# Two-layer encoder trunk: row norm ahead of the MLP's joins, sums that begin with the residual, operand differences on the vector engine

## The chip, the cores and the metric

One core of a Trainium2 chip runs the whole program. The metric is the device time in microseconds (us) of one execution. The engines are TensorE (PE, with its weight load PEld), VectorE (DVE), ScalarE (ACT), GpSimd (POOL) and SyncE (SP, which issues the DMAs).

## The reference

A trunk of two layers over a sequence of 1024 tokens with 1024 channels, all float32:

```
per layer:
  h = RMSNorm(x);  z = h @ W_in
  mix = concat[ attention(z), gated recurrence(z), conv module(z) ]
  x = x + mix @ W_out
  x = x + relu(RMSNorm(x) @ W1)^2 @ W2        # W1: 1024x4096, W2: 4096x1024
RMSNorm(x) = x * rsqrt(mean(x*x) + 1e-6) * gain
```

The change touches the last line only, the MLP.

## The kernel before, in words

**Arithmetic.** Tiles have channels on the 128 partitions and tokens along the row. Each float32 operand of a matmul is split into a high part (ACT, a rounding copy) and a low part (DVE, operand minus high part); `parts` does both (L900 to 910). A product takes three passes (high-high, high-low, low-high), so a product of one 128x512 result over four 128-row steps is 12 matmuls of 128x512.

**Two halves.** The MLP of a layer is done with seven products M1 to M7 in place of eight, in the manner of Strassen. The first half (x to hidden) runs 16 pairs p of hidden tiles times seven products in the order M1, M5, M2, M3, M6, M4, M7 (`product`, matmul L1009); the first two pairs are interleaved. The second half (hidden to output) runs 4 groups sg times seven stages in the order M1, M2, M5, M6, M3, M7, M4, and each stage four output tiles dt of 12 matmuls (matmul L1217). Both halves hold 28 x 48 = 1344 matmuls of 128x512.

**Operand sums and differences.** Before they are split, operands are combined: `sub` (L918), `add` (L915) and the sum for M5 in `parts` (L906) run on POOL; four differences of x per product M5 and M6 run on DVE. The functions are `x_parts` and `w_split`.

**Joins.** In the first half, `join` adds two partial results (DVE, L1018), then ACT does Relu (L1019) and Square (L1020). For pairs 12 to 15 DVE then multiplies with the row norm (`scaled`, L996). Differences t1, t2 (DVE) and t3, t4 (POOL) of the results are stored to memory with them (`store_half`, L921), for the second half to read back.

**Row norm.** The square of the norm's inverse can be taken out of relu(.)^2, so `sum_rows` (all-ones matmul L271) is called behind product 18 and its reciprocals behind products 40 to 47, and the hidden tiles of pairs 0 to 11 are not scaled: their sums are, in group sg 2 of the second half, on POOL (L996), where POOL also adds the residual (L915), which `residual` (L1157) fetches into buffers "m".

**Second half.** `load2` (L1063) loads W2 tiles, `load_a` (L1070) the stored activations, `collect` takes results out of PSUM: the first of each accumulator an ACT copy, the others a DVE add (L1194).

**What sets the order.** A scheduler orders instructions on each engine by program order, priority and its own costs, and gives any free buffer of a pool (14 buffers "m", 16 "xs", 8 "x", 4 "tmp"). Inside `ordered`, instructions of an engine are held in the order of the program: separate chains "a" (ACT), "v" (DVE), "p" (POOL) at the start of the first half, and a new chain from 4 products before its end through the second half; in between there is none. Parts are made 4 products (later 4 to 8 tiles) ahead of the matmuls.

Of the kernel before, what the change touches and what calls it, by code (L numbers as in the profile page):

```python
# [17 lines left out]
P = 128  # L18
# [27 lines left out]
def tile_hybrid_trunk(  # L46
# [128 lines left out]
    def flip(w, half):  # L175
        b = pse()
# [51 lines left out]
    def norm_stats(ssq):  # L228
        sp = pse()
# [5 lines left out]
        for h in range(2):  # L235
            nc.scalar.activation(rb[:, h * 512 : (h + 1) * 512], flip(w, h), AF.Copy)
        return rc, rb

    class Norm:
# [22 lines left out]
        def done(self):  # L262
            self.rc, self.rb = norm_stats(self.ssq)
            return self.rc, self.rb

        def sum_rows(self):
            all_ones = tmp((P, P))
            nc.gpsimd.memset(all_ones, 1.0)
            for half in halves(self.ssq):
                s = pse()  # L270
                nc.tensor.matmul(s, all_ones, half, start=True, stop=True)  # L271
                nc.scalar.activation(half, s, AF.Copy)
            return self.ssq
# [21 lines left out]
    for l in range(DEPTH):  # L295
# [574 lines left out]
        norm = Norm(lambda k: None, sp_.t([P, L], "Rb"))  # L870
# [62 lines left out]
        def x_parts(name):  # L933
# [8 lines left out]
            elif name == "M5":  # L942
                BC[name] = []
                for kt in R4:
                    nc.vector.tensor_tensor(B[1][kt], B[2][kt], B[1][kt], op=ALU.subtract)
                    BC[name].append(parts(B[1][kt], b_t()))
            elif name == "M3":
                BC[name] = [parts(B[4][kt], m_t()) for kt in R4]
            elif name == "M6":
                for kt in R4:  # L950
                    sub(B[2][kt], B[4][kt], B[2][kt])
                    nc.vector.tensor_tensor(B[4][kt], B[4][kt], B[1][kt], op=ALU.subtract)
# [8 lines left out]
        def w_split(name, a11, a12, a21, a22, box):  # L961
            if name == "M3":
                sub(a12, a12, a11)
            src = {"M1": a11, "M2": a12, "M5": (a21, a22), "M6": a11, "M3": a12, "M4": a22, "M7": a21}[name]
            both = parts(src, box)
            if name == "M5":
                sub(a21, a11, a21)
                sub(a11, a22, a21)
            return both
# [25 lines left out]
        def scaled(eng, dst, src, h):  # L995
            eng.tensor_tensor(dst, src, r2[:, h * 512 : (h + 1) * 512], op=ALU.mult)  # L996

        def product(p, name):
# [17 lines left out]
            def join(m, h, a, b):  # L1016
                o = d["o"][m][:, h * 512 : (h + 1) * 512]
                nc.vector.tensor_tensor(o, a, b, op=ALU.add)  # L1018
                nc.scalar.activation(o, o, AF.Relu)  # L1019
                nc.scalar.activation(o, o, AF.Square)  # L1020
                if p >= NPAIR - SG:
                    scaled(nc.vector, o, o, h)
                return o

            with tc.high_priority() if p == NPAIR - 1 else nullcontext():
# [3 lines left out]
                elif name == "M2":  # L1029
                    d["o"] = [spare(p), spare(p)]  # L1030
                    store_half(p, "M1", join(0, 0, bank, d["m1"]))
# [4 lines left out]
                elif name == "M6":  # L1036
                    b11, b12 = halves(d["o"][0])
                    join(0, 1, bank, d["m1"])
# [17 lines left out]
        seq = [(p, n) for n in ORDER[:5] for p in range(2)] + [(p, n) for p in range(2) for n in ORDER[5:]]  # L1056
# [9 lines left out]
        def load_a(sg, name):  # L1066
            for h in range(2):
                t = m_t() if sg > 0 or name not in ("M1", "M2") else b_t() if name == "M1" else tmp()
# [31 lines left out]

# [205 lines left out]
```

## Time and profile before

| | |
|---|---|
| median of 3 runs | 2584.42 us (2583.92 to 2586.57) |
| profiled execution | 2586.23 us, span 2584.3 us |
| PE busy in the span | 95% |
| DVE, ACT, POOL busy | 76%, 50%, 45% |
| MLP, first half, layers 0 and 1 | 318.29 and 318.35 us |
| MLP, second half, layers 0 and 1 | 324.66 and 325.79 us |
| mean granted clock in these | 0.97 to 0.99 |

The halves run from one first matmul to the next half's (the last one to its last matmul). Besides its 1344 matmuls each holds a few others. The profile counts an engine as busy while it executes, not while it waits for a semaphore.

### The profile page before, as it was taken

Reading aid. Unit: us, or ns where it says so; the run is one execution under the profiler, and the core shown is the slowest. Engines: PE = TensorE matmul, PEld = TensorE weight load, DVE = VectorE, ACT = ScalarE, POOL = GpSimd, SP = SyncE. Lnnn points to the kernel's source line nnn. Section 1 sums busy time; section 2 is a strip of 40 time slices with the busy share of each in tenths; the row PEclk is TensorE's granted clock in tenths of the full one; section 3 lists DMA queues with packets and bytes.
Section 4 is the critical chain, followed back from the end, with each engine's and each line's share of the span. In section 5 each row is a group of like instructions: output and inputs, shape, how many; then the busy total and the mean of one; then the engine's idle time right before and its main releaser. Section 6 shows DMA issues by size and latency. Waiting matters only on the chain. (4 is left out here: it accounts for less than half of the span.)

```text
span 2584.3 us, 34195 instructions
## 1 busy us (share of the span) xinstructions
PE 2463.8 (95%) x12568; PEld 2026.7 (78%) x12568; DVE 1971.8 (76%) x2725; ACT 1291.1 (50%) x2118; POOL 1159.5 (45%) x735
## 2 busy tenths in 40 slices
PE   8989999999999999999899899999998999999998
PEld 7767788878788887888787777888786888878886
DVE  6998589862865578899859985998628655788996
ACT  4222478763655555433423225777636555554322
POOL 0232566533644434357423325664346354343581
PEclk9999999999999999999999999999999999999999
DMA  4101300032244457445231112000323443664343
GB/s 162 52 33 59 106 24 18 26 128 93 91 162 147 163 186 245 134 144 172 101 109 44 48 61 96 17 22 22 133 88 118 147 163 139 217 219 156 113 163 122
DMA packets 115127, 287.01 MB, mean 111 GB/s; under 512 B 11408, under 2 KB 11664, under 8 KB 114960
## 3 DMA queue, kind: packets, MB, share of 16 engines
q1 hardware_dynamic: 114960, 284.83, 32.1%
q8 instruction: 99, 1.62, 0.3%
q14 instruction: 68, 0.56, 0.1%
HBM read 197.75 MB, written 87.03 MB: 110 GB/s over the span
## 5 line engine op out<-in xcount | busy, mean ns | idle before, releaser
L223 PE MATMUL S<-xs,whi 128*128 128x512 f32 x1280 | 363.6, 405 | 10.0 <-ACT xs L208 8.5
L223 PEld LDWEIGHTS S<-xs,whi 128*128 128x128 f32 x1280 | 243.1, 193 | 66.2 <-ACT xs L208 8.5
L908 ACT ACTIVATE xs<-m 128x512 fp32r<-128x512 f32 x216 | 125.8, 620 | 206.4 <-issue 52.7
L909 DVE TENSOR_TENSOR xs<-m,xs 128x512 fp32r<-128x512 f32 x216 | 207.3, 984 | 18.7 <-ACT xs L908 18.7
L769 POOL TENSOR_SCALAR P<-P,mx 128x1024 f32<-128x1024 f32 x124 | 143.0, 1153 | 164.6 <-DVE mx L768 122.1
L223 PE MATMUL S<-xs,wlo 128*128 128x512 f32 x640 | 203.0, 398 | 0.0
L1217 PE MATMUL S<-xs,xs 128*128 128x512 f32 x816 | 200.5, 389 | 0.0
L795 DVE TENSOR_TENSOR PT<-c,PT 128x512 fp32r<-128x512 f32 x256 | 170.9, 683 | 23.6 <-ACT PT L794 22.0
L794 ACT ACTIVATE PT<-c 128x512 fp32r<-128x512 f32 x256 | 147.5, 593 | 69.3 <-PE c L790 66.2
L199 ACT ACTIVATE whi<-raw 128x1024 fp32r<-128x1024 f32 x56 | 59.1, 1057 | 246.1 <-PE S L223 233.2
L1217 PEld LDWEIGHTS S<-xs,xs 128*128 128x128 f32 x816 | 153.2, 188 | 31.8
L811 PE MATMUL e<-PT,x 128*128 128x256 f32 x1024 | 173.2, 299 | 1.6 <-ACT PT L794 1.3
L764 DVE TENSOR_SCALAR_CACHE_REDUCE P<-S,nqc 128x1024 f32<-128x1024 f32 x124 | 158.4, 1278 | 16.1 <-PE S L753 7.2
L360 DVE SCALAR_TENSOR_TENSOR x<-x,par,x 128x1009 f32<-128x1009 f32 (+14 forms) x120 | 166.5, 1387 | 1.8
L790 PE MATMUL c<-cons,P 128*128 128x128 f32 x992 | 152.1, 277 | 10.4 <-POOL P L769 5.3
L753 PE MATMUL S<-x,QS 128*128 128x512 f32 x480 | 155.6, 423 | 4.7 <-DVE P L764 4.5
L1217 PE MATMUL c<-xs,xs 128*128 128x512 f32 x552 | 143.1, 405 | 13.3 <-DVE x L1194 13.1
L767 ACT ACTIVATE P<-P,mx 128x1024 f32<-128x1024 f32 x124 | 142.5, 1149 | 24.2 <-DVE P L764 22.7
L811 PEld LDWEIGHTS e<-PT,x 128*128 128x128 f32 x1024 | 139.5, 193 | 10.3 <-ACT PT L794 3.7
L1217 PE MATMUL e<-xs,xs 128*128 128x512 f32 x552 | 137.5, 391 | 9.7 <-DVE xs L909 6.6
L790 PEld LDWEIGHTS c<-cons,P 128*128 128x128 f32 x992 | 115.3, 141 | 36.3 <-issue 10.5
L223 PEld LDWEIGHTS S<-xs,wlo 128*128 128x128 f32 x640 | 122.6, 192 | 26.8 <-issue 0.3
(314 smaller groups left out, 5960.4 us busy)
## 6 DMA issues: line engine op xcount, KB each, us to landing
m<-ad SPq DMA_DIRECT2D x104, 512.0 KB, 3.9
ad<-x SPq DMA_DIRECT2D x176, 256.0 KB, 2.1
raw<-w_in_t SPq DMA_DIRECT2D x40, 512.0 KB, 3.4
xs<-w_t SPq DMA_DIRECT2D x36, 512.0 KB, 3.8
raw<-w_t SPq DMA_DIRECT2D x36, 512.0 KB, 3.5
m<-w_t SPq DMA_DIRECT2D x32, 512.0 KB, 4.9
ad<-tmp SPq DMA_DIRECT2D x48, 256.0 KB, 2.0
x<-w_t SPq DMA_DIRECT2D x24, 512.0 KB, 5.7
```

Of the source, the lines that this page charges most:

```text
L223: nc.tensor.matmul(zp[h] if type(zp) is list else zp[:, h, :], w, xx[:, h * 512 : (h + 1) * 512], start=first, stop=last)
L360: nc.vector.scalar_tensor_tensor(y[:, lo:hi], u[:, lo + d : hi + d], par[:, l, wof + tap : wof + tap + 1], y[:, lo:hi], op0=ALU.mult, op1= ...
L753: nc.tensor.matmul(S[:, hb, :], qs, kk[:, hb * 512 : (hb + 1) * 512], start=first, stop=not first)
L764: nc.vector.tensor_scalar(Pt, S, nqc[:, j, ci : ci + 1], 3.0e38, op0=ALU.mult, op1=ALU.min, accum_out=mx[:, 1:2])
L767: nc.scalar.activation(Pt, Pt, AF.Exp, bias=mx[:, 1:2], scale=-1.0, accum_out=mx[:, 2:3])
L769: nc.gpsimd.tensor_scalar(Pt, Pt, mx[:, 3:4], 0.0, op0=ALU.mult, op1=ALU.add)
L790: nc.tensor.transpose(t[:, q * P : (q + 1) * P], Pt[:, hb, q * P : (q + 1) * P], ident)
L794: nc.scalar.activation(hi, src, AF.Copy)
L795: nc.vector.tensor_tensor(lo, src, hi.bitcast(F32), op=ALU.subtract)
L811: nc.tensor.matmul(pvp[:, cs], VS[g][:, hb * 4 + kb, :], pt[:, kb, :], start=hb == 0 and n == 0, stop=hb == 1 and n == 7,)
L909: ordered("v", nc.vector.tensor_tensor(lo, src, hi.bitcast(F32), op=ALU.subtract))
L1217: nc.tensor.matmul(banks[dt], w[i][:, dt * P : (dt + 1) * P], a[j], start=n == 0 and name not in ("M6", "M7", "M3"), stop=n == 3 * SG - 1, ...
```

## The change

- The row norm is computed at the start of the first half: `norm.square` of the last x tile on DVE behind product 0, `norm.done` behind product 2. That is eight small column sums on PE (written in two parts, 16 matmuls of 128x1), 12 DVE operations of 128x8, an ACT widening, 8 PE transposes and 2 ACT copies into the tile `Rb`. `sum_rows`, the reciprocals and `scaled` are gone.
- A join is now a DVE add, a DVE `scalar_tensor_tensor` (max with 0, times `Rb`) and an ACT Square; the Relu is gone. For M2 of pairs 0 and 1 the second and third step come later, at M6.
- The accumulators of the second half are loaded with the residual (`load_acc`, 8 tiles of 0.5 MB), four behind the last but one product of the first half and four at the start of the second; every `collect` is a DVE add, and the POOL scaling and adding in sg 2 is gone.
- `add` and `sub` run on the engine in `row[0]`: DVE for the first 11 products, POOL up to 14 products before the first half's end, DVE from there and through the second half. They stand in the DVE chain "v" with the low parts. t3 and t4 follow `row[0]`.
- The two interleaved pairs at the start come in another order: M1 M1 M5 M5, then M2 M3 of pair 0, M2 M3 of pair 1, M6 M6, M4 M7, M4 M7.
- In group 0 of the second half the activations of M2 lie in buffers "xs", where they lay in "tmp".

```diff
-            if type(src) is tuple:
-                s = tmp((P, 512))
-                ordered("p", nc.gpsimd.tensor_tensor(s, *src, op=ALU.add))
-                src = s
...
+        row = [nc.vector]
...
-            nc.gpsimd.tensor_tensor(dst, a, b, op=ALU.add)
+            ordered("v", row[0].tensor_tensor(dst, a, b, op=ALU.add))
...
-            ordered("p", nc.gpsimd.tensor_tensor(dst, a, b, op=ALU.subtract))
+            ordered("v", row[0].tensor_tensor(dst, a, b, op=ALU.subtract))
...
-            def join(m, h, a, b):
+            def join(m, h, a, b, then):
                 o = d["o"][m][:, h * 512 : (h + 1) * 512]
                 nc.vector.tensor_tensor(o, a, b, op=ALU.add)
-                nc.scalar.activation(o, o, AF.Relu)
-                nc.scalar.activation(o, o, AF.Square)
-                if p >= NPAIR - SG:
-                    scaled(nc.vector, o, o, h)
+
+                def finish():
+                    r = norm.rb[:, h * 512 : (h + 1) * 512]
+                    nc.vector.scalar_tensor_tensor(o, o, 0.0, r, op0=ALU.max, op1=ALU.mult)
+                    nc.scalar.activation(o, o, AF.Square)
+                    if then:
+                        store_half(p, then, o)
+
+                if p < 2 and name == "M2":
+                    d["late"] = finish
+                else:
+                    finish()
                 return o
...
-                    nc.gpsimd.tensor_tensor(t3, b22, b12, op=ALU.subtract)
-                    nc.gpsimd.tensor_tensor(t4, b21, t2, op=ALU.subtract)
+                    row[0].tensor_tensor(t3, b22, b12, op=ALU.subtract)
+                    row[0].tensor_tensor(t4, b21, t2, op=ALU.subtract)
...
-        seq = [(p, n) for n in ORDER[:5] for p in range(2)] + [(p, n) for p in range(2) for n in ORDER[5:]]
+        seq = [(p, n) for ns in (("M1",), ("M5",), ("M2", "M3"), ("M6",), ("M4", "M7")) for p in range(2) for n in ns]
...
+        def load_acc(m, dt):
+            acc[m, dt] = x8() if m == 0 else m_t()
+            nc.sync.dma_start(acc[m, dt], xmd[4 * m + dt])
...
             if k == 14 - AHEAD:
                 chain = None
+                row[0] = nc.gpsimd
+            if k == len(seq) - 14:
+                row[0] = nc.vector
+            if k == 0:
+                norm.square(xt, nc.vector)
             if k == 2:
-                norm.square(xt)
-            if k == 18:
-                r2 = norm.sum_rows()
...
+                norm.done(ps2())
...
-                    if (m, h, dt) not in seen:
-                        seen.add((m, h, dt))
-                        nc.scalar.activation(sl, src, AF.Copy)
-                        continue
                     with tc.high_priority():
-                        nc.vector.tensor_tensor(sl, sl, src, op=ALU.add)
-                    if sg == NG - 2 and LAST.get(name) == (m, h):
-                        scaled(nc.gpsimd, sl, sl, h)
-                        add(sl, sl, res[m, h][dt])
+                        nc.vector.tensor_tensor(quad(m, h, dt), quad(m, h, dt), banks[dt], op=ALU.add)
```

**DVE at the start of layer 1's first half.** The first rows behind the last x tile (the add into "tmp"). Before, low parts of x into "xs" and "m" and of W1 into "whi" and "wlo":

```order
L1105 TENSOR_TENSOR tmp_16044<-tmp_16044,S_2623_16046 128x1024
L909 TENSOR_TENSOR xs_16159<-x_2607_15861,xs_16159 128x512
L909 TENSOR_TENSOR xs_16162<-x_2613_15924,xs_16162 128x512
L909 TENSOR_TENSOR xs_16165<-x_2619_15987,xs_16165 128x512
L909 TENSOR_TENSOR xs_16168<-x_2624_16095,xs_16168 128x512
L909 TENSOR_TENSOR whi_16171<-raw_16096,whi_16171 128x512
L909 TENSOR_TENSOR wlo_16193<-xs_16100,wlo_16193 128x512
L909 TENSOR_TENSOR m_16211<-x_2607_15861,m_16211 128x512
```

The same place of the changed kernel, from the second low part of "m" on (the twelve rows ahead of it are the same kind of low parts and one add of 128x1024 for the norm):

```order
L897 TENSOR_TENSOR m_16163<-x_2620_16053,m_16163 128x512
L907 TENSOR_TENSOR raw_16054<-raw_16054 128x512
L151 TENSOR_SCALAR nwa_16212<-S_2659_16202 128x8
L152 TENSOR_SCALAR nwy_16213<-nwa_16212 128x8
L154 SCALAR_TENSOR_TENSOR nwt_16214<-nwy_16213 128x8
L155 TENSOR_TENSOR nwt_16214<-nwt_16214,nwa_16212 128x8
L897 TENSOR_TENSOR wlo_16166<-raw_16054,wlo_16166 128x512
L897 TENSOR_TENSOR whi_16185<-xs_16058,whi_16185 128x512
L156 SCALAR_TENSOR_TENSOR nwy_16213<-nwt_16214,nwy_16213 128x8
L907 TENSOR_TENSOR xs_16058<-xs_16058 128x512
```

The differences of W1 (L907), which stood on POOL, stand between the low parts (L897), and the norm's small operations (L151 to 156) between these.

**DVE at the transition to layer 1's second half.** Before, the low parts for stage M2 ("xs" from "m" or "tmp", then "whi" and "wlo") and the first of M5 ("xs" from "tmp", which holds the sum for M5, and from "m"), up to the first collect:

```order
L909 TENSOR_TENSOR xs_18700<-m_18633,xs_18700 128x512
L909 TENSOR_TENSOR xs_18701<-tmp_18639,xs_18701 128x512
L909 TENSOR_TENSOR whi_18706<-m_18635,whi_18706 128x512
L909 TENSOR_TENSOR wlo_18707<-tmp_18639,wlo_18707 128x512
L909 TENSOR_TENSOR xs_18728<-tmp_18730,xs_18728 128x512
L909 TENSOR_TENSOR xs_18729<-m_18684,xs_18729 128x512
L909 TENSOR_TENSOR xs_18754<-tmp_18756,xs_18754 128x512
L1194 TENSOR_TENSOR x_2985_18750<-x_2985_18750,e_18802 128x512
L909 TENSOR_TENSOR xs_18755<-m_18684,xs_18755 128x512
```

Changed, from the first sum for M5 (L904) on, which stands behind M2's low parts and the last joins of pair 15 (L1175 are collects: "S" holds results of stage M1, "e" and "c" the four results of M2):

```order
L904 TENSOR_TENSOR tmp_18702<-raw_18412,m_18587 128x512
L907 TENSOR_TENSOR raw_18412<-raw_18412 128x512
L907 TENSOR_TENSOR raw_18412<-m_18587,raw_18412 128x512
L897 TENSOR_TENSOR xs_18700<-tmp_18702,xs_18700 128x512
L1175 TENSOR_TENSOR x_2970_18615<-x_2970_18615,S_2977_18655 128x512
L1175 TENSOR_TENSOR x_2968_18611<-x_2968_18611,e_18770 128x512
L1175 TENSOR_TENSOR x_2971_18617<-x_2971_18617,S_2977_18655 128x512
L1175 TENSOR_TENSOR x_2969_18613<-x_2969_18613,c_18771 128x512
L1175 TENSOR_TENSOR x_2970_18615<-x_2970_18615,e_18772 128x512
L1175 TENSOR_TENSOR x_2971_18617<-x_2971_18617,c_18773 128x512
L897 TENSOR_TENSOR xs_18701<-m_18656,xs_18701 128x512
L904 TENSOR_TENSOR tmp_18726<-raw_18414,m_18589 128x512
```

The collects of M2's four results, which stood among and behind the parts of M5, stand ahead of them, all but the first operand's; and M5's sums and differences (L904, L907), which stood on POOL, stand on DVE.

**SP at the same transition.** Changed: the accumulators' loads (L1098, from the residual `xmd`) and those of the activations of M5 and M6 (L1063, from `ad`):

```order
L910 DMA ad_75<-x_2960_18583 128x512
L910 DMA ad_75<-x_2961_18584 128x512 x2
L1098 DMA m_18650<-xmd_74 128x1024
L1098 DMA m_18652<-xmd_74 128x1024
L1063 DMA m_18656<-ad_75 128x2x512
L1063 DMA m_18658<-ad_75 128x2x512
L1063 DMA m_18696<-ad_75 128x2x512
```

Before, L1070 loads of the activations followed the stores at once; the residual's loads (L1157) stood in sg 2.

## Rows read from the trace of the kernel before

**Rows 1.** The page's busy times of the engines, with their shares of the span and instructions.

```profile
PE 2463.8 (95%) x12568; PEld 2026.7 (78%) x12568; DVE 1971.8 (76%) x2725; ACT 1291.1 (50%) x2118; POOL 1159.5 (45%) x735
```

**Rows 2.** Busy time by stretch: layer 0's first and second half of the MLP, then layer 1's. Columns: the stretch, its length, busy us (and instructions) of PE, PEld, DVE, ACT, POOL, the granted clock as a share of full speed, the DMA engines' share and GB/s.

```profile
651.72:970.01 318.29, 311.94 (x1350) 255.74 (x1348) 219.16 (x266) 186.71 (x329) 151.76 (x101) 0.98 0.44 153
970.01:1294.67 324.66, 311.64 (x1346) 255.15 (x1344) 287.74 (x339) 141.55 (x251) 166.49 (x102) 0.97 0.48 160
1936.31:2254.66 318.35, 310.66 (x1350) 254.34 (x1348) 218.94 (x265) 186.70 (x329) 151.42 (x101) 0.99 0.44 153
2254.66:2580.45 325.79, 311.30 (x1345) 254.73 (x1343) 277.03 (x332) 127.26 (x236) 157.43 (x98) 0.98 0.46 159
```

**Rows 3.** The same view of layer 1's second half by group: sg 0, 1, 2 and 3.

```profile
2254.66:2340.24 85.58, 79.33 (x338) 64.28 (x336) 73.25 (x86) 47.02 (x88) 38.46 (x25) 0.96 0.63 209
2340.24:2416.40 76.16, 76.16 (x338) 63.06 (x336) 62.16 (x86) 30.23 (x57) 25.93 (x16) 1.00 0.44 152
2416.40:2493.00 76.60, 75.73 (x333) 62.09 (x332) 75.73 (x84) 27.03 (x51) 55.20 (x35) 1.00 0.50 172
2493.00:2580.45 87.45, 80.08 (x342) 65.29 (x340) 65.89 (x80) 22.99 (x43) 37.84 (x24) 0.96 0.29 105
```

**Rows 4.** Timeline of PE at the start of layer 1's first half: start, us, engine, line, operation, out and in, count, and in brackets the idle time ahead of it with what ended it. The first row is the first product of pair 0, the row of 1985.07 the first of pair 2; L271 is the all-ones matmul.

```profile
1936.31 2.88 PE L1009 MATMUL c<-xs,whi 128*128 128x512 f32 x12
...
1959.40 2.56 PE L1009 MATMUL e<-m,wlo 128*128 128x512 f32 x10 [3.14 <-DVE wlo L909]
...
1966.88 4.64 PE L1009 MATMUL c<-m,whi 128*128 128x512 f32 x10 [3.00 <-DVE whi L909]
...
1985.07 2.88 PE L1009 MATMUL c<-xs,whi 128*128 128x512 f32 x12
...
1999.47 1.88 PE L271 MATMUL e<-Rb,tmp 128*128 128x512 f32 x4
```

**Rows 5.** Timelines of DVE and POOL in the same stretch, and one POOL row late in the first half, while DVE runs no operation on two SBUF operands (2230.71). L909 are low parts (two operands in SBUF), L918 differences on POOL.

```profile
1940.90 2.50 DVE L909 TENSOR_TENSOR xs<-x,xs 128x512 fp32r<-128x512 f32 x4 [1.74 <-ACT xs L908]
1944.99 6.50 DVE L909 TENSOR_TENSOR m<-x,m 128x512 fp32r<-128x512 f32 x4 [0.31 <-ACT m L908]
```

```profile
1947.50 6.83 POOL L918 TENSOR_TENSOR x<-x,x 128x512 f32<-128x512 f32 x4
...
2230.71 1.29 POOL L918 TENSOR_TENSOR xs<-xs 128x512 f32<-128x512 f32 x1 [1.58 <-DVE wlo L909]
```

**Rows 6.** Groups of instructions in sg 1 of layer 1's second half (2340.24 to 2416.40): busy us, mean ns, idle time ahead. First DVE (low parts, then a collect from a PSUM bank "S"), then POOL.

```profile
L909 DVE TENSOR_TENSOR xs<-m,xs 128x512 fp32r<-128x512 f32 x27 | 22.3, 851 | 4.0 <-ACT xs L908 4.0
...
L1194 DVE TENSOR_TENSOR x<-x,S 128x512 f32<-128x512 f32 x8 | 5.1, 676 | 0.0
...
L909 DVE TENSOR_TENSOR whi<-m,whi 128x512 fp32r<-128x512 f32 x3 | 2.0, 681 | 0.0
```

```profile
L906 POOL TENSOR_TENSOR tmp<-x,m 128x512 f32<-128x512 f32 x4 | 7.0, 1759 | 58.6 <-DVE xs L909 58.6
```

**Rows 7.** The whole run's largest group of low parts, in the same form.

```profile
L909 DVE TENSOR_TENSOR xs<-m,xs 128x512 fp32r<-128x512 f32 x216 | 207.3, 984 | 18.7 <-ACT xs L908 18.7
```

**Rows 8.** Timeline of PE at the transition to layer 1's second half (the rows that waited for DVE are M2's), and the stretch in their midst by engine (columns as in Rows 2).

```profile
2254.66 2.20 PE L1217 MATMUL S<-xs,xs 128*128 128x512 f32 x9
...
2267.64 0.97 PE L1217 MATMUL e<-xs,xs 128*128 128x512 f32 x3 [1.04 <-DVE xs L909]
2271.01 0.73 PE L1217 MATMUL e<-xs,xs 128*128 128x512 f32 x2 [2.40 <-DVE xs L909]
...
2274.38 1.22 PE L1217 MATMUL e<-wlo,whi 128*128 128x512 f32 x2 [2.41 <-DVE wlo L909]
```

```profile
2272.00:2276.00 4.00, 1.62 (x4) 1.34 (x5) 4.00 (x4) 1.15 (x2) 3.84 (x4) 0.50 1.06 395
```

**Rows 9.** Timelines of sg 2 and 3 of layer 1's second half: two PE rows, then all engines around the longest wait (a scaling and a residual add on POOL, ACT's high part, DVE's low parts and the collect that PE waited for).

```profile
2517.53 2.30 PE L1217 MATMUL e<-xs,xs 128*128 128x512 f32 x9 [1.59 <-DVE x L1194]
...
2526.29 4.21 PE L1217 MATMUL c<-xs,xs 128*128 128x512 f32 x9 [5.78 <-DVE x L1194]
```

```profile
2516.20 1.72 POOL L915 TENSOR_TENSOR m<-m,m 128x512 f32<-128x512 f32 x1
...
2519.12 1.28 POOL L996 TENSOR_TENSOR m<-m,Rb 128x512 f32<-128x512 f32 x1
...
2519.98 0.63 ACT L908 ACTIVATE xs<-m 128x512 fp32r<-128x512 f32 x1 [14.15 <-DMA m<-ad]
...
2522.23 1.74 DVE L909 TENSOR_TENSOR xs<-x,xs 128x512 fp32r<-128x512 f32 x1
2523.50 1.59 POOL L915 TENSOR_TENSOR m<-m,m 128x512 f32<-128x512 f32 x1
2523.89 1.74 DVE L909 TENSOR_TENSOR xs<-m,xs 128x512 fp32r<-128x512 f32 x1
...
2525.56 0.68 DVE L1194 TENSOR_TENSOR x<-x,c 128x512 f32<-128x512 f32 x1
```

**Rows 10.** Timeline of the same norm steps where the kernel before has them, in layer 1's first projection: column sums, the last of 12 small DVE operations, the widening, the transposes, and the copies to `Rb`.

```profile
1306.91 1.84 PE L162 MATMUL e<-cons,tmp 128*128 128x1 f32 x16
...
1311.00 0.17 DVE L232 COPY Rc<-nwy 128x8 f32<-128x8 f32 x1
...
1311.26 1.06 ACT L168 ACTIVATE tmp<-Rc 128x1024 f32<-128x1024 f32 x1 [4.91 <-DVE Rc L232]
...
1312.38 1.08 PE L178 MATMUL e<-cons,tmp 128*128 128x128 f32 x8
...
1313.07 1.09 ACT L236 ACTIVATE Rb<-e 128x512 f32<-128x512 f32 x2 [0.75 <-PE e L178]
```

More of the change, by code (lines that the diff above doesn't have):

```diff
@@ L173, in widen, with flip @@
         return w.rearrange("p a b c -> p a (b c)")
-    def flip(w, half):
-        b = pse()
+    def flip(w, half, b=None):
+        b = pse() if b is None else b
         for q in range(4):
@@ L260, in square, with done @@
             self.sums += 1
-        def done(self):
-            self.rc, self.rb = norm_stats(self.ssq)
+        def done(self, bank=None):
+            self.rc, self.rb = norm_stats(self.ssq, bank)
             return self.rc, self.rb
[L266 to L273, printed above, removed]
     def halves(t):
@@ L869, in tile_hybrid_trunk @@
         xT = []
-        norm = Norm(lambda k: None, sp_.t([P, L], "Rb"))
+        norm = Norm(lambda k: None)
         for j in range(KT):
@@ L942, in x_parts @@
             elif name == "M5":
-                BC[name] = []
                 for kt in R4:
-                    nc.vector.tensor_tensor(B[1][kt], B[2][kt], B[1][kt], op=ALU.subtract)
-                    BC[name].append(parts(B[1][kt], b_t()))
+                    sub(B[1][kt], B[2][kt], B[1][kt])
+                BC[name] = [parts(B[1][kt], b_t()) for kt in R4]
             elif name == "M3":
@@ L963, in w_split @@
                 sub(a12, a12, a11)
-            src = {"M1": a11, "M2": a12, "M5": (a21, a22), "M6": a11, "M3": a12, "M4": a22, "M7": a21}[name]
-            both = parts(src, box)
+            src = {"M1": a11, "M2": a12, "M6": a11, "M3": a12, "M4": a22, "M7": a21}.get(name)
             if name == "M5":
+                src = tmp((P, 512))
+                add(src, a21, a22)
                 sub(a21, a11, a21)
                 sub(a11, a22, a21)
-            return both
+            return parts(src, box)
         wflip = [0]
@@ L1030, in product @@
                     d["o"] = [spare(p), spare(p)]
-                    store_half(p, "M1", join(0, 0, bank, d["m1"]))
+                    join(0, 0, bank, d["m1"], "M1")
                 elif name == "M5":
@@ L1037, in product @@
                     b11, b12 = halves(d["o"][0])
-                    join(0, 1, bank, d["m1"])
+                    d.pop("late", lambda: None)()
+                    join(0, 1, bank, d["m1"], None)
                     d["t"] = halves(x8()) + halves(x8())
@@ L1067, in load_a @@
             for h in range(2):
-                t = m_t() if sg > 0 or name not in ("M1", "M2") else b_t() if name == "M1" else tmp()
+                t = b_t() if sg == 0 and name in ("M1", "M2") else m_t()
                 q = sg * SG + 2 * h
@@ L1143, in tile_hybrid_trunk @@
                 AS[0, "M2"] = list(load_a(0, "M2"))
+            if k == len(seq) - 2:
+                for dt in R4:
+                    load_acc(0, dt)
         if not last_l:
             norm = Norm(lambda k: pv(l + 1, "nmix", k))
-        acc = {}
+        for dt in R4:
+            load_acc(1, dt)
         def quad(m, h, dt):
             return acc[m, dt][:, h * 512 : (h + 1) * 512]
-        def residual(m, h):
-            for i in range(2):
-                t = m_t()
-                k = 4 * m + 2 * i
-                nc.sync.dma_start(
-                    t.rearrange("p (q t) -> p q t", q=2),
-                    xmd[k : k + 2, :, h * 512 : (h + 1) * 512].rearrange("q p t -> p q t"),
-                )
-                yield from halves(t)
         stages = [(sg, n) for sg in range(DFF // P // 2 // SG) for n in NAMES]
```

31 lines of the change are left out of this document (9 added, 22 removed).

## The prediction

> **What bounds the kernel now.** I read the page's busy times first: PE is busy for 95% of the span, so time can only be won where PE waits or runs at the lower clock [rows 1]. The change touches the MLP alone, so next come the four halves of the MLP by stretch [rows 2]. What would each take without a stall? Group sg 1 of layer 1 is the yardstick: 336 matmuls in 76.16 us, PE busy throughout at a granted clock of 1.00 [rows 3], which is 0.227 us a matmul, 2.72 us a product of 12 and 304.64 us a half of 1344. Against that the first halves lose 13.65 and 13.71 us, the second halves 20.02 and 21.15 us [rows 2]: 68.5 us in all, which is the most that the change could give if it adds nothing.
>
> Where the losses lie, from the timelines of layer 1 (layer 0 has nearly the same lengths):
> A, the start of the first half. Fourteen products stand between the first product of pair 0 and that of pair 2, 38.08 us of work; they took 1985.07 - 1936.31 = 48.76 us, a loss of 10.68. The two rows with waits of 3.14 and 3.00 us wait for low parts of W1 from DVE [rows 4]. The rest is the clock, which falls to half behind such gaps (the row behind the second gap took 4.64 us for 10 matmuls). The all-ones matmuls add 1.88 us later [rows 4].
> B, sg 0 of the second half: 85.58 - 76.16 = 9.42 us [rows 3], in M2's rows that wait for low parts, 1.04, 2.40 and 2.41 us; in the midst of it the granted clock is 0.50, DVE is busy for all of 4.00 us with four instructions, POOL for 3.84 [rows 8].
> C, sg 2 and 3: 0.44 and 11.29 us [rows 3], most of it one wait of 5.78 us for a collect on DVE and the half clock behind it [rows 9].
>
> All three have one cause in the rows. A DVE operation on two SBUF operands takes 2.50 / 4 = 0.62 us while POOL stands still, and 6.50 / 4 = 1.62 while POOL runs; POOL takes 1.29 alone and 6.83 / 4 = 1.71 beside DVE [rows 5]. The two together take as long as one after the other. A collect with its operand in PSUM stays at 0.68 [rows 6, 9]. Within one stage the same low parts show both sides: 851 ns on average where POOL ran sums, 681 where it did not [rows 6].
>
> **The change part by part.**
>
> Operand sums and differences to DVE. Each costs DVE 0.62 us and takes a POOL operation away that stretched DVE's work by some 1.0 us (1.62 - 0.62) [rows 5]. In the second half a group has 56 low parts, 16 sums and differences and 32 collects: 104 operations, 72 x 0.62 + 32 x 0.68 = 66.4 us, by the unpaired duration of 681 ns [rows 6] 70.8. The stage has 76.16. So DVE would be 87 to 93% busy; sg 1 ran without loss at 82%, and sg 2, at 75.73 busy of 76.60, lost 0.44 [rows 3]. I take it that a group in the middle loses nothing.
>
> The Trainium skill speaks against this edit: "Perfetto Trace Analysis", section Optimizing Scalar/DVE Operations, says that with a saturated DVE some work may go to ScalarE or even GpSimd, the reverse of what is done here; it adds that the two share an SBUF read port, so that moving work between them might not help. "SBUF — State Buffer", section Who interferes with whom, calls that port an exclusive lock, and the trace agrees (1.62 beside POOL, 0.62 alone). By the first sentence alone the move would load the busier engine, with the end that R2 gives; by the second the lock is what is saved.
>
> A, the start. Behind the last x tile DVE now has, up to the last W1 part of pair 1: 48 operations of 128x512 (low parts, the differences of x and W1, a few joins), two of 128x1024 and the norm's 12 small ones, by the order of the changed kernel. That is 48 x 0.62 + 2 x 1.25 (twice the former) + 12 x 0.2 (0.17 a row, with a gap, [rows 10]) = 34.7 us, less than PE's 38.08, so DVE keeps ahead if POOL is silent. PE gains the norm's column sums and transposes, 1.84 + 1.08 = 2.9 us [rows 10]. Does their chain stop PE? The sums wait for a square made on DVE behind product 0; the transposes wait for DVE's 12 operations among low parts (some 2.4 us plus six low parts of 0.62) and ACT's 1.06 us; PE has products between them. Walking the two orders against each other, with these durations, puts pair 2's first product 42.2 us behind the first of pair 0: a loss of 4.1 (2.9 of new work, 1.2 of waits) where it was 10.7. Bounds: 2.9 if nothing waits, 8 if the transposes wait for the whole chain and the clock falls. With the all-ones matmuls gone (1.9), and what is left of the 13.7 staying, the first half loses 4.7 instead: **-9.0 us a layer**.
>
> Joins. The step on two SBUF operands is DVE's, 16 of the 64 joins had one already; 64 a layer at the 984 ns of the mixed group [rows 7] are 63 us, less the 16 of `scaled`, about 47 us more on top of 219 of 318 [rows 2]. That leaves DVE at 84%, spread over 16 pairs of 19 us with parts made four products ahead. I cost it at nothing; without that slack (above 304 us busy) it would come out of PE time one for one. Relu leaves ACT (busy 187 of 318 [rows 2]), which is not late anywhere but in A.
>
> B, the transition. POOL is silent now, so M2's parts run at 0.62 instead of 1.62 or more, and M2's waits (5.85 us and the clock behind them) go. But M5's parts come late: DVE's order, which is held, has all but one of them behind the collects of M2's four results. So M5 starts about 0.9 us behind M2's end, and each of its four operand pairs needs five DVE operations, 3.1 us, where PE uses 48 / 4 matmuls = 2.72. PE's order takes the four results in turn, and DVE is done 15.5 operations, 9.6 us, after that start; the 13 or so matmuls that then remain take 3.0 us. M5 ends 0.9 + 9.6 + 3.0 = 13.5 us behind M2 instead of 10.88: 2.6 lost, and 0.5 more for M6. I take 3.2 of loss against 9.4: **-6.1 a layer**. Bounds: 1.5 with M5's high parts early enough to fill the start; 9 if the clock falls to half.
> Data. The accumulators bring 8 loads of 0.5 MB to the transition, 4.2 MB, six ahead of M5's activations on SP's queue. At the 395 GB/s of [rows 8] they take 10.6 us. M5's activations can be asked for only when pair 15 frees an "m" buffer, some 5 us ahead of the transition, and are wanted 22 us behind it: hidden, with about 10 us to spare.
> The ACT copies that began the sums become 32 DVE adds a layer in sg 0, counted above.
>
> C. The POOL scaling and adding (1.3 to 1.7 us each, 64 a run) is gone, and with it the buffers "m" that the residual held until POOL had added it: ACT's part waited 14.15 us for a DMA into such a buffer, then DVE's low parts ran at 1.74, and the collect that PE waited for stood behind them [rows 9]. Neither cause is left. 0.44 + 11.29 = 11.7, in layer 0, whose half loses 1.1 less [rows 2], about 10.8; I leave 0.5: **-10.8 a layer**. Bounds: 0 to 2 left.
>
> Sum: 9.0 + 6.1 + 10.8 = 25.9 a layer, 51.7 us in both. From the profiled execution, 2586.23 (span 2584.3, the rest around it), that is **2534.5 us**; the median of the runs is 1.8 below the profiled one, which I don't subtract, since the profile after will carry its own. By the bounds the sum runs from 2 x (5.1 + 0.4 + 9.3) = 30 to 2 x (10.2 + 7.9 + 11.3) = 59 us: 2527 to 2556.
>
> **The rivals.**
> R1, the transition keeps its stall: M5's parts behind M2's collects and the 4.2 MB cost what M2's waits did. For: the held order, and a DMA system that was full there (395 GB/s) [rows 8]. Against: the count above. B then loses 9.4 to 12: 2547 to 2552.
> R2, slower: DVE becomes the bound in the second half. If low parts keep their 984 ns [rows 7] with POOL silent, because the stretch has another cause, a group needs 72 x 0.984 + 32 x 0.68 = 92.6 us, a half 370; against a mean of 325.2 that adds 45 a layer, and with A's gain 2586.2 + 90.4 - 18 = 2659. It decides from a mean of 76.16 / 104 = 0.73 us an operation. Against: 681 and 851 ns side by side in one stage [rows 6].
> R3, the norm's chain stops PE at the start: M2 of pair 1 and what follows wait for `Rb` or for a PSUM bank, and A loses 10.7 + 2.9 as before: 2534.5 + 19 = 2553.5. For: a chain over PE, DVE, ACT, PE and ACT among held orders. Against: the late finish of M2's joins.
> R4, it does not do what it says: the waits were of buffers and DMAs (C's 14.15 us), and others take their place at all three: within 5 us of before.
>
> **How the numbers follow.** Forecast (2523 to 2544) 0.64; R1 0.14; R3 0.11; R1 and R3 together, about 2568, 0.03; R2 0.05; R4 0.03. The likeliest gives 2534.5. The range takes in R1 and R3 and, below, stalls that all go, with only the norm's 2 x 2.9 us added: 2586.2 - 68.5 + 5.8 = 2523.5. So 2523 to 2556, with some 0.13 outside. A measurement of this kernel can tell about 0.2% (5 us) from no change: faster 0.92, same 0.03, slower 0.05.
>
> **What would show it.** Right: second halves of 308 to 310 us with a granted clock near 1.00, DVE 62 to 71 us busy in each of sg 1 and 2, low parts at a mean of 0.62 to 0.69, no PE wait above 1 us in sg 2 and 3; pair 2's first product 41 to 44 us behind pair 0's; M5's rows in sg 0 with waits of a few tenths up to 1 us. Wrong: low parts near 0.98 with POOL idle (R2), PE rows that wait for transposes or for a bank held by a join at the start (R3), M5 waiting for a DMA or for more than 3 us in all (R1). The forecast fails most likely at B, whose number rests on a walk by hand.

## The result and the profile after

| | before | changed |
|---|---|---|
| median | 2584.17 us (4 runs, 2582.18 to 2586.57) | 2547.51 us (4 runs, 2543.57 to 2551.20) |
| profiled execution | 2586.23 us, span 2584.3 | 2548.54 us, span 2546.8 |
| ratio changed / before | | 0.9858 (95%: 0.9846 to 0.987) |

The kernel became 1.4% faster, 37 us, inside the range (2523 to 2556) but 13 us behind the 2534.5 forecast (14 by the profiled execution, from which the forecast was counted). The page's busy times after, against [rows 1]:

```profile
PE 2451.1 (96%) x12608; PEld 2020.0 (79%) x12608; DVE 2003.2 (79%) x3023; ACT 1202.9 (47%) x1960; POOL 779.0 (31%) x491
```

DVE has 298 instructions more and only 31 us more work. The four halves of the MLP and layer 1's groups, in the columns of [rows 2, 3]:

```profile
649.98:965.33 315.35, 309.40 (x1370) 254.39 (x1369) 248.48 (x325) 149.51 (x266) 123.19 (x80) 1.00 0.45 156
965.33:1276.41 311.08, 307.75 (x1346) 253.12 (x1345) 268.38 (x422) 133.61 (x234) 9.57 (x4) 0.99 0.49 166
1916.05:2230.95 314.90, 309.34 (x1369) 254.32 (x1368) 248.87 (x325) 150.10 (x266) 121.66 (x80) 1.00 0.45 156
2230.95:2542.90 311.95, 307.69 (x1345) 252.75 (x1343) 256.62 (x415) 119.42 (x219) 0.00 (x0) 0.99 0.47 164
2230.95:2314.42 83.47, 79.21 (x337) 63.64 (x336) 71.53 (x117) 36.40 (x67) 0.00 (x0) 0.98 0.70 250
2314.42:2390.58 76.16, 76.16 (x337) 63.11 (x336) 68.41 (x112) 31.57 (x58) 0.00 (x0) 1.00 0.49 166
2390.58:2466.74 76.16, 76.16 (x337) 63.10 (x336) 60.59 (x98) 29.01 (x54) 0.00 (x0) 1.00 0.41 145
2466.74:2542.90 76.16, 76.16 (x337) 62.91 (x335) 56.09 (x91) 22.43 (x41) 0.00 (x0) 1.00 0.25 87
```

Against 304.64 us a half the first halves now lose 10.71 and 10.26 us (before 13.65 and 13.71), the second 6.44 and 7.31 (20.02 and 21.15). Groups 1 to 3 lose nothing at all: C is gone to the last tenth. What is left of the second half is in group 0, and the first half has kept three quarters of its loss. The low parts, once 984 ns [rows 7]:

```profile
L897 DVE TENSOR_TENSOR xs<-m,xs 128x512 fp32r<-128x512 f32 x216 | 144.9, 694 | 24.8 <-ACT xs L896 24.8
```

The start of layer 1's first half on PE, against [rows 4] (L162 and L178 are the norm's; the row of 1961.43 is pair 2's first product):

```profile
1924.21 1.84 PE L162 MATMUL S<-cons,tmp 128*128 128x1 f32 x16
...
1947.41 3.02 PE L995 MATMUL S<-m,whi 128*128 128x512 f32 x12 [0.59 <-DVE whi L897]
1951.62 0.96 PE L995 MATMUL S<-m,whi 128*128 128x512 f32 x3 [1.19 <-DVE whi L897]
...
1961.43 2.97 PE L995 MATMUL c<-xs,whi 128*128 128x512 f32 x12 [1.81 <-DVE tmp L1004]
...
1970.74 3.02 PE L995 MATMUL e<-m,wlo 128*128 128x512 f32 x12 [0.90 <-ACT tmp L1027]
...
1980.58 1.66 PE L995 MATMUL c<-m,whi 128*128 128x512 f32 x6 [1.06 <-DVE tmp L1004]
```

Pair 2 starts 45.38 us behind pair 0: 7.30 lost where 4.1 was forecast. A new wait ends that stretch, for a join (L1004) that has not yet freed a PSUM bank, and two more follow within pair 2: one for a copy on ACT (L1027) and one for a join. Why is the join late? DVE and POOL at that moment:

```profile
1953.29 0.68 DVE L1008 SCALAR_TENSOR_TENSOR x<-x,Rb 128x512 f32<-128x512 f32 x1
1953.89 0.68 DVE L1004 TENSOR_TENSOR x<-c,tmp 128x512 f32<-128x512 f32 x1
1954.49 1.60 DVE L1035 TENSOR_TENSOR x<-tmp 128x512 f32<-128x512 f32 x1
1956.02 1.77 DVE L1008 SCALAR_TENSOR_TENSOR x<-x,Rb 128x512 f32<-128x512 f32 x1
...
1958.92 1.76 DVE L1035 TENSOR_TENSOR x<-x 128x512 f32<-128x512 f32 x1
1960.60 0.68 DVE L1004 TENSOR_TENSOR tmp<-c,tmp 128x512 f32<-128x512 f32 x1
```

```profile
1954.25 1.29 POOL L904 TENSOR_TENSOR tmp<-raw 128x512 f32<-128x512 f32 x1 [43.96 <-DMA raw<-w_t]
1955.62 1.62 POOL L907 TENSOR_TENSOR raw<-raw,raw 128x512 f32<-128x512 f32 x1
```

POOL wakes at 1954.25 with the differences that `row[0]` gives back to it, and DVE's steps on two SBUF operands (L1008, L1035) go from 0.68 to 1.60 and 1.77 us just ahead of the join; the joins themselves (L1004), with one operand in PSUM, stay at 0.68.

The transition, against [rows 8]: M2's waits are gone, save 1.21 us at its start (in layer 0 that one too); M5 waits in their place.

```profile
2256.45 0.49 PE L1195 MATMUL e<-xs,xs 128*128 128x512 f32 x1 [2.00 <-ACT xs L896]
2257.18 0.73 PE L1195 MATMUL e<-xs,xs 128*128 128x512 f32 x2 [0.23 <-DVE xs L897]
...
2259.02 0.80 PE L1195 MATMUL e<-xs,xs 128*128 128x512 f32 x1 [0.65 <-ACT xs L896]
```

ACT and SP show what M5 waited for:

```profile
2237.08 0.63 ACT L896 ACTIVATE xs<-xs 128x512 fp32r<-128x512 f32 x1 [4.75 <-DMA xs<-ad]
...
2255.77 0.63 ACT L896 ACTIVATE xs<-m 128x512 fp32r<-128x512 f32 x1 [6.99 <-DMA m<-ad]
```

```profile
2234.62 1.47 SPq L1098 DMA_DIRECT2D m<-xmd  x2
2245.13 3.06 SPq L910 DMA_DIRECT2D ad<-x  x5
2248.28 1.19 SPq L1098 DMA_DIRECT2D m<-xmd  x2
2249.56 11.20 SPq L1063 DMA_DIRECT2D m<-ad  x7
```

M5's activations (L1063) were asked for at 2249.56, 18.6 us behind the transition, because on SP's queue they follow two accumulator loads (L1098), and these follow pair 15's last stores (L910), which wait for its last joins, which stand in DVE's order behind parts of M2, whose activations came at 2237.08. The other two loads of the lower accumulators had gone out at 2234.62, ahead of the stores.

### The profile page after: what moved, and what is told of

The parts are those of the page before. It is cut to its first block, busy times and chain, and to the rows that moved or that the text cites. A ratio compares the mean times of both kernels' runs of the same rounds, so it can differ in the third digit from the quotient of the medians.

```text
span 2546.8 us, 34055 instructions
## 1 busy us (share of the span) xinstructions
PE 2451.1 (96%) x12608; PEld 2020.0 (79%) x12608; DVE 2003.2 (79%) x3023; ACT 1202.9 (47%) x1960; POOL 779.0 (31%) x491
## 3 DMA queue, kind: packets, MB, share of 16 engines
q8 instruction: 99, 1.62, 0.3%
## 4 chain that ended last, share of the span: by engine, by line
PE 77%; DVE 14%; ACT 3%; issue 2%; POOL 2%; DMA 1%; SPq 0%; DVEq 0%; ACTq 0%; POOLq 0%
PE S L223 15%; PE S L1195 10%; PE c L995 9%; PE e L1195 7%; PE c L1195 6%; PE e L995 6%; PE S L995 6%; DVE x L352 4%; PE e L803 4%; PE c L782 3%; PE S L745 3%; PE e L494 2%; PE e L162 1%; PE e L583 1%; DVE P L756 1%
## 5 line engine op out<-in xcount | busy, mean ns | idle before, releaser
L897 DVE TENSOR_TENSOR xs<-m,xs 128x512 fp32r<-128x512 f32 x216 | 144.9, 694 | 24.8 <-ACT xs L896 24.8
L260 POOL TENSOR_TENSOR tmp<-tmp,tmp 128x1024 f32<-128x1024 f32 x19 | 50.6, 2664 | 364.4 <-ACT tmp L259 364.2
L782 PE MATMUL c<-cons,P 128*128 128x128 f32 x992 | 151.9, 277 | 10.5 <-POOL P L761 5.6
L1195 PE MATMUL e<-xs,xs 128*128 128x512 f32 x552 | 142.9, 395 | 7.2 <-ACT xs L896 6.8
```

The lines of the kernel that those rows point to most:

```text
L782: nc.tensor.transpose(t[:, q * P : (q + 1) * P], Pt[:, hb, q * P : (q + 1) * P], ident)
L897: ordered("v", nc.vector.tensor_tensor(lo, src, hi.bitcast(F32), op=ALU.subtract))
L1195: nc.tensor.matmul(banks[dt], w[i][:, dt * P : (dt + 1) * P], a[j], start=n == 0 and name not in ("M6", "M7", "M3"), stop=n == 3 * SG - 1, ...
```

## The experiments

My theory: POOL's silence is the gain; the 13 us are lost because POOL comes back at pair 2, and because M5's data are asked for late. Rivals: the engine of the differences is of no account (residual and norm bring the gain); the norm's chain stops PE; DVE's own queue is too long. The rows come from several chips; the kernel before took 2584.2 to 2585.8 us on them. Group 0 loses 4.5 to 8.5 us in the rows that leave the transition as changed (changed, changed again, 3, 5, 6, 7, 10), so a difference inside that says nothing. Losses below are a half's length less 304.64 us, or group 0's less 76.16, layer 0 / layer 1; "C" is groups 1 to 3.

| run | median us | first half | group 0 | C |
|---|---|---|---|---|
| before | 2584.2 | 13.65 / 13.71 | 9.18 / 9.42 | 10.84 / 11.73 |
| changed | 2547.5 | 10.71 / 10.26 | 6.44 / 7.31 | 0 / 0 |
| changed again | 2550.1 | 10.38 / 10.36 | 8.49 / 5.13 | 0 / 0 |
| 1 sums on POOL | 2579.8 | 16.06 / 16.00 | 17.16 / 15.77 | 0.2 / 0.3 |
| 2 sums on DVE alone | 2554.5 | 9.15 / 9.12 | 2.62 / 0.86 | 9.82 / 8.44 |
| 3 no norm | 2544.0 | 7.84 / 8.46 | 6.58 / 5.86 | 0 / 0 |
| 4 accumulators late | 2541.7 | 11.00 / 10.35 | 2.62 / 3.14 | 0 / 0 |
| 5 switch late | 2536.7 | 5.34 / 5.30 | 8.28 / 6.13 | 0 / 0 |
| 6 Relu on ACT | 2542.9 | 6.77 / 6.83 | 5.59 / 8.49 | 0 / 0 |
| 7 M4 M4 M7 M7 | 2547.5 | 9.77 / 9.72 | 4.47 / 5.96 | 0 / 0 |
| 8 = 4 + 5 | 2530.6 | 5.38 / 5.33 | 2.95 / 2.43 | 0 / 0 |
| 9 = 4 + 5 + 7 | 2531.0 | 4.39 / 4.39 | 2.42 / 2.41 | 0 / 0 |
| 10 POOL silent | 2539.9 | 5.36 / 5.33 | 5.61 / 6.72 | 0 / 0 |

**1. Sums and differences back on POOL.**

```diff
...
-            ordered("v", row[0].tensor_tensor(dst, a, b, op=ALU.subtract))
+            ordered("p", nc.gpsimd.tensor_tensor(dst, a, b, op=ALU.subtract))
...
```

> The changed kernel with the operand sums and differences back on POOL as in the kernel before (four differences of x in M5 and M6 on DVE, the rest on POOL in a chain of its own), t3 and t4 on POOL too; norm, joins and sums that begin with the residual stay as changed. Theory (DVE and POOL share their way to SBUF, and the gain comes from POOL falling silent where PE has no slack): A and B lose what they lost before or more, since the norm's and the joins' operations are added, 11 to 16 us in A and 9 to 13 in B a layer, low parts near 0.98 us on average; C stays without loss, since no residual is added there and no buffer is held. Some 2565 to 2580 us. Rival (the gain is that of the residual and the norm alone, the engine of the differences is of no account): 2545 to 2550, A and B as in the changed kernel, 7 and 7 us.

Ratio to before 0.9982 (0.9973 to 0.9992): the rest of the change, without the sums on DVE, brings 5 us. Some 22 us in both layers are won in C and most of them lost again, 4.7 in the first halves and 14.3 in group 0, where the loss of 16 to 17 us is above the 9 to 13 expected. The stall at M5 is larger, since its activations were asked for 29 us behind the transition, and PE waits for the norm too:

```profile
1963.90 1.11 PE L178 MATMUL S<-cons,tmp 128*128 128x128 f32 x4 [4.36 <-ACT tmp L168]
...
2290.36 4.23 PE L1193 MATMUL e<-xs,xs 128*128 128x512 f32 x9 [6.45 <-ACT xs L896]
```

The rival falls. So does a part of my reasoning on A: the norm's chain does stop PE, by 1.95 and 4.36 us, once DVE's steps are stretched. C loses 0.2 to 0.3 with the sums on POOL: by themselves they cost nothing there. Low parts took 887 ns on average, where 980 was expected.

**2. The sums on DVE alone, in the kernel before.**

```diff
...
+        row = [nc.vector]
...
-            ordered("p", nc.gpsimd.tensor_tensor(dst, a, b, op=ALU.subtract))
+            ordered("v", row[0].tensor_tensor(dst, a, b, op=ALU.subtract))
...
```

> The kernel before with one part of the change alone: operand sums and differences on DVE in the low parts' chain for the first 11 products, in the last 14 and in the second half, t3 and t4 along with them. Norm, joins, residual, order of the first products as before. Theory: A falls from 10.7 to about 4 to 6 us of loss (no norm work there), B from 9.4 to 2 to 5 (no accumulator loads ahead of M5's activations), C keeps a stall, since POOL still scales and adds 32 tiles a layer and holds the residual's buffers: 5 to 12 of its 11.7. Some 2555 to 2568 us. Rival (C's stall came from POOL sums beside low parts alone): C falls to under 2 and the time to 2540 to 2550.

0.9885 (0.9869 to 0.9902): 30 of the 37 us. A falls to 4.4, group 0 to 2.6 and 0.9. C falls by 1.0 and 3.3 and otherwise stays, with the wait it had in [rows 9]:

```profile
2490.34 4.17 PE L1221 MATMUL e<-xs,xs 128*128 128x512 f32 x9 [5.37 <-DVE x L1198]
```

Hence the parts of the gain: A and B are the sums', C in the main that of the scaling and the residual taken off POOL. In B the whole change loses 4 to 6 us a layer more than this run (6.44 and 7.31); run 4 shows what of that its loads cost. Did C come from POOL's work beside DVE or from the buffers that the residual held? Ahead of that wait POOL scales and adds without a pause up to 2482.54; DVE's low part takes 1.78 us until then and 0.69 behind it, and ACT waits for DVE's sum, not for a DMA as it did in [rows 9]:

```profile
2479.61 1.78 DVE L909 TENSOR_TENSOR xs<-m,xs 128x512 fp32r<-128x512 f32 x1
2480.91 1.63 POOL L916 TENSOR_TENSOR m<-m,m 128x512 f32<-128x512 f32 x1
...
2483.30 0.63 ACT L908 ACTIVATE xs<-tmp 128x512 fp32r<-128x512 f32 x1 [7.45 <-DVE tmp L906]
...
2483.97 0.69 DVE L909 TENSOR_TENSOR xs<-tmp,xs 128x512 fp32r<-128x512 f32 x1 [0.78 <-ACT xs L908]
```

So in run 2 the longest wait comes from POOL's work beside DVE. What the held buffers cost in the kernel before was not taken apart.

**3. No norm in the MLP.**

```diff
-            if k == 0:
-                norm.square(xt, nc.vector)
-            if k == 2:
-                norm.done(ps2())
+            if k == 0:
+                norm.rb = sp_.t([P, L], "Rb")
+                nc.gpsimd.memset(norm.rb, 0.5)
```

> The changed kernel without the norm's computation in the MLP: the last square, the column sums, the 12 small DVE operations, the widening, the transposes and the copies are left out, and the tile the joins multiply with is filled with a constant by POOL, so the MLP's result is not normalised. Theory (at the start DVE is the engine that ends last, and the norm's 3.6 us on it and 2.4 us on PE are paid in full): A falls from 7.3 to 2 to 4 us of loss, 7 to 11 us in both layers, 2537 to 2541. Rival (the norm is hidden but for PE's 2.4 us): A falls to 4.9, 2543. Rival (its PSUM bank or its tile Rb delays the joins and through them pair 2): A and the waits behind it, 10.3 in all, fall to under 4: 2533 to 2536.

Pair 2 starts 42.95 us behind pair 0 (1914.93 to 1957.88) instead of 45.38: 2.43 less, which is the norm's time on PE. The wait for the join stays, 1.93. The first rival has it: hidden but for PE's work; neither the theory's 3 to 5 us nor a bank. R3 of the prediction falls with it, as long as POOL is silent.

**4. Lower accumulators late.**

```diff
-        for dt in R4:
-            load_acc(1, dt)
...
+            if k == 1:
+                for dt in R4:
+                    load_acc(1, dt)
```

> The changed kernel with the loads of the four lower accumulators moved from the start of the second half to its second stage, behind the loads of the activations of M5 and M6. Theory (M5's start waits for its activations, which stand behind two of these loads and the last stores on SP's queue): the wait of 2.0 to 2.3 us at M5's start falls to under 1 and B from 6.4 to 7.3 us of loss to 4 to 5.5, some 4 us in both layers: 2542 to 2545. Rival (DVE's order, with the parts of M5 behind the collects of M2, sets M5's start): B stays within 0.7 us of 6.4 and 7.3. Rival (the stores ahead, which wait for pair 15's last joins on DVE, set the issue): the activations are issued within 1 us of where they were, and B falls by 0 to 1.

M5's first activations are now asked for at 2233.83:

```profile
2231.28 2.45 SPq L1098 DMA_DIRECT2D x<-xmd  x4
2233.83 1.44 SPq L1063 DMA_DIRECT2D m<-ad  x2
2244.29 2.88 SPq L910 DMA_DIRECT2D ad<-x  x5
```

Group 0 loses 2.62 and 3.14, M5's wait of 2 us is gone: M5 starts as M2 ends. It gained more than the theory gave, and both rivals fall. What is left has the size of the prediction's walk by hand (3.2) but not its place: the walk had M5 start 0.9 us late, while the largest wait now is M6's, for a low part (1.33 in layer 0):

```profile
2268.25 2.11 PE L1195 MATMUL S<-xs,xs 128*128 128x512 f32 x8 [1.29 <-DVE xs L897]
```

The edit takes the loads away ahead of M5's data both from SP's queue and from the DMA engines, so it does not tell which of the two held the data up more. In the scheduler's order on DVE it also moved a low part and a sum of M5 ahead of M2's last collect.

**5. Switch to POOL ten products later.**

```diff
             if k == 14 - AHEAD:
                 chain = None
+            if k == 20:
                 row[0] = nc.gpsimd
```

> The changed kernel with the operand sums and differences of the first half on DVE ten products longer (POOL takes them from behind product 20 instead of 10). Theory (when the third pair starts, its PSUM bank waits for a join on DVE, which is late because POOL's first differences stretch DVE's steps to 1.6 to 1.77 us just then): the wait of 1.8 to 2.2 us ahead of pair 2 falls to under 1, and those of 0.9 and 1.06 behind it shrink; the first half loses 8 to 9.3 instead of 10.3 to 10.7, some 3 us in both layers. Rival (DVE is late by its own queue): the waits stay within 0.4 us or grow, as pair 2 and 3 add some 8 operations each to DVE; no gain or a loss of up to 4 us.

2536.74 against 2550.11 of the changed kernel on the same chip: 10.1 us of it are the first halves', and 2.9 lie in the stretch ahead of the MLP (649.21 against 652.14), which the edit does not touch. All waits for joins and copies behind the start are gone, 5 us a layer where 1.5 was expected; the two for low parts of M4 stay:

```profile
1947.41 0.96 PE L995 MATMUL S<-m,whi 128*128 128x512 f32 x3 [1.17 <-DVE whi L897]
```

DVE at the same point as above, POOL asleep till 1972.58:

```profile
1950.28 0.68 DVE L1035 TENSOR_TENSOR x<-tmp 128x512 f32<-128x512 f32 x1
1950.88 0.68 DVE L1008 SCALAR_TENSOR_TENSOR x<-x,Rb 128x512 f32<-128x512 f32 x1
```

Every step is 0.68, and the last join of the first two pairs starts 49.2 us behind pair 0's first product where it started 49.9 behind it, although DVE now does pair 2's sums and differences among them.

**6. The join's added step left out.**

```diff
-                    r = norm.rb[:, h * 512 : (h + 1) * 512]
-                    nc.vector.scalar_tensor_tensor(o, o, 0.0, r, op0=ALU.max, op1=ALU.mult)
+                    nc.scalar.activation(o, o, AF.Relu)
```

> The changed kernel with the join's step on two SBUF operands left out: Relu on ACT as before, no product with the norm, which is still computed and used by nothing, so the MLP's result is not normalised. DVE loses 64 operations a layer. Theory (the join's added step costs only where DVE is behind, at pairs 0 to 3): the waits for the joins ahead of pair 2 (1.8 to 2.2) and behind it (1.06) fall to under 0.5, the first half loses 7 to 8.5 instead of 10.5, and from pair 4 on nothing changes; 4 to 7 us in both layers. Rival (hidden everywhere): within 1 us a layer. Rival (DVE at 79% of the first half is late here and there): the stretch from pair 4 to the end, which lost under 0.6, gains nothing either way, so it can only show in a larger gain ahead of it.

The first half loses 6.8, the waits for joins are gone, one of 1.60 for a copy stays. So the added step costs 3.5 us a layer when POOL is awake. With POOL asleep it leaves no wait for a join (run 5, which keeps it, loses 5.3); no run takes it out there. The gains of runs 5 and 6 are not to be added: both take away the wait ahead of pair 2.

**7. M4 M4 M7 M7.**

```diff
-... ("M6",), ("M4", "M7")) ...
+... ("M6",), ("M4",), ("M7",)) ...
```

> The changed kernel with the last four products of the first two pairs in the order M4 M4 M7 M7 instead of M4 M7 M4 M7. Theory (PE waits twice at the start, 0.6 and 1.2 us, for low parts of W1 of M4, the second because pair 1's stands in DVE's order behind all parts of M7): the second wait goes, a shorter one at M7 comes in its place, A falls by 0.5 to 1.5 us a layer, 1 to 3 us in all. Rival (DVE's work as a whole ends last, whatever the order): A within 0.4 us.

The wait of 1.2 us goes, one of 0.5 at M7 comes, and the first half gains 0.6 us a layer against the changed kernel on the same chip; the wait for a join in pair 2's M7 grows from 1.06 to 2.41. In the time this cannot be told from no change.

**Changed again, and 8 to 10.**

> The changed kernel once more, unaltered, so that the three that follow are compared with it on one chip: 2543 to 2551 us, losses of 10 to 11 us in each first half and 6 to 8 in each second.

> The changed kernel with both edits that gained: operand sums on DVE up to product 20, and the four lower accumulators loaded behind the activations of M5 and M6. Theory (the two stalls are apart, one at the start of the first half, one at the transition): losses of 5.3 in the first halves and 2.5 to 3.5 in the second, 16 to 18 in all; from 2536.7 and the 4 us of a layer that B gave, 2528 to 2532 us. Rival (what is won at the start is partly waited for at the transition): 2534 to 2538.

> The same two edits and the order M4 M4 M7 M7 in the first two pairs. Theory (with the late switch, the waits for the joins are gone, and what is left at the start is the norm's 2.4 us on PE and two waits of 0.6 and 1.2 for low parts of M4, of which this order takes the second): the first halves lose 4 to 5 instead of 5.3, 1 to 2 us less than the run beside it. Rival (the wait moves to M7): within 1 us of it.

> The changed kernel with the operand sums on DVE throughout, so that POOL does nothing in the MLP but the norm's squares of the neighbouring stages. Theory (DVE at 0.62 to 0.68 us an operation holds all of it: per pair 7 low parts, 8 steps of joins, 4 differences of results and 4 of W1, 23 x 0.65 = 15 of 19 us): first halves lose 5 to 5.8, as with the late switch, 2535 to 2539 us. Rival (DVE becomes the bound in the middle of the first half): the stretch from pair 4 on loses several us more, 2545 or above.

Runs 4 and 5 add up, in the losses as in the time: run 8 is 2530.61 us, 0.9797 (0.978 to 0.9814) of before, the best version with run 9 beside it (2530.99): the waits that run 7's order takes, 1 us a layer, show in the trace but not in the time. Run 10 shows how much room DVE has: the stretch from pair 2 to the end of the first half with POOL at zero:

```profile
1955.00:2225.00 270.00, 270.00 (x1192) 223.72 (x1192) 207.54 (x331) 124.01 (x218) 0.00 (x0) 1.00 0.50 175
```

331 DVE operations in 207.54 us, 0.63 each, PE without a gap. The first halves lose what they lose in run 5: nothing in them needs POOL, nor gains by it. The time, 2539.9, is 1 us above the range expected.

## Why the prediction was right, and where it was off

**The cause held.** DVE's work on two SBUF operands, 0.62 us alone and 1.62 beside POOL, was the basis of all three terms; for A and B runs 1, 2, 5 and 10 show it from four sides, for C the trace of run 2 does. R2 (DVE as the bound, 2659) did not come: low parts took 694 ns, and DVE was busy 56 to 72 us in a group. The time itself fell into R1's band (2547 to 2552) and not into the forecast's own (2523 to 2544): it is inside the range because the range took in R1 and R3. It got there by two shortfalls, in A and in B; R1's loss of 9.4 to 12 in B alone did not come. Of the signs, low parts and groups 1 to 3 came as said; the second halves (311.1 and 312.0 us against 308 to 310) and pair 2's first product (45.4 against 41 to 44) missed theirs, and M5's wait for a DMA, a sign of R1, came.

**C: -10.8 a layer forecast, -10.8 and -11.7 measured.** Right, and by the scaling and the residual, as said (runs 1 and 2).

**A and the rest of the first half: -9.0 forecast, -2.9 and -3.4 measured.** The term that failed is the first half's loss of 4.7, which came to 10.5: 5.8 us too little a layer, 11.6 of the error. Of this 0.5 a layer is a slip in the sum: 4.1, and the 1.1 that 10.7 and 1.9 leave of 13.7, make 5.2 and a gain of 8.5. Its condition, "if POOL is silent", I took as met up to pair 2. It was not: the parts of pair 2 and after are POOL's, made four products ahead, and so fall on the joins of pairs 0 and 1. Run 5 keeps POOL away and loses 5.3, close to the sum, though by other parts: pair 2 starts 5.3 us late instead of 4.1, and nothing is lost behind it. With it failed "I cost it at nothing" for the join's added step: as an average (84% busy forecast, 79% measured) it was hidden, at pairs 0 to 3 it was not (run 6, 3.5 us). A second, smaller fault: I set DVE's whole work, 34.7 us (measured: busy 33.35 of the 36.52 us from 1916.25 to 1952.77), against PE's 38.08 and took it as in time. Each part is due when its own product starts, M4's from 27 us on, and there PE waited 0.6 and 1.2 us.

**The norm's price, 2.9 us of PE work: 2.4 measured** (run 3); the chain beside it cost nothing.

**B: -6.1 forecast, -2.7 and -2.1 measured.** Here the step on the data failed, "hidden, with about 10 us to spare". I set the time of M5's loads by the buffer alone, 5 us ahead of the transition; they were issued 18.6 us behind it, since SP's queue stood behind stores that wait for joins that DVE's order holds behind M2's parts. That is R1, in part: by its DMAs, not by DVE's order, for with the loads behind M5's data group 0 lost 2.6 to 3.1 (run 4). That the walk had said 3.2 is luck in part: M5 starts on time there, and M6 waits.

**The sum.** 2534.5 + 11.6 (first half) + 7.4 (B, 2 x 3.7) - 1.0 (C's 0.5 twice) = 2552.5; the profiled run took 2548.54. The rest, 3.9, lies outside the MLP: the stretch ahead of layer 0's first half was 1.7 us shorter than before, that between the layers 2.0, and both move by this much where nothing in them differs (the first is 649.98 and 652.14 in two runs of the changed kernel, the second 639.2 to 641.5 over all runs), so it is no effect of the change that these runs show. Without it the forecast would have been off by 18 us, not by 14.

## What to carry to other kernels

Where two engines stretch each other's work, moving work from the slow one to the fast one can pay even though the fast one is busier; but cost it by the stretch in which the slow one is really silent, and look for the point at which it wakes. A late engine is judged by the due time of each piece, not by its total against the other's total. And for a load that is moved or added, follow its queue back to what the entries ahead of it wait for: a buffer that is free early helps nothing behind a store that waits for a join.

## What the hardware showed that I had not expected

POOL can be held up far more than DVE. Side by side, each took 1.6 to 1.7 us an operation before [rows 5] (four of each in 6.5 to 6.8 us, a little under the 2.50 + 4 x 1.29 = 7.7 of one after the other). In run 5, where DVE was busy 20.73 of the 21.00 us from 1957 to 1978, its steps kept 0.68 and POOL's first two operations took 3.97 and 6.52:

```profile
1972.58 3.97 POOL L904 TENSOR_TENSOR tmp<-raw 128x512 f32<-128x512 f32 x1 [66.45 <-DVE xs L907]
1976.63 6.52 POOL L907 TENSOR_TENSOR raw<-raw,raw 128x512 f32<-128x512 f32 x1
```

What decides which of the two gives way, these runs don't show.

The clock did not fall behind the short gaps at the start (granted 1.00 from 1916.05 to 1982, with waits of 0.59, 1.19 and 1.81 us), but at M5, where a wait of 2.00 us was followed by single matmuls between further waits, it was 0.76 on average from 2257 to 2260; before, gaps of 3.0 us were followed by rows at half speed [rows 4]. The length of a gap alone does not tell: ahead of pair 2 a wait of 1.93 us was followed by a granted clock of 1.00 in run 3 and of 0.72 over the next 6 us in the repeat of the changed kernel.
